# Splitting ordinary weight pieces with a casting and an accumulating DMA instead of VectorE's subtraction

## The chip, the cores and the metric

The kernel runs on one core of one Trainium2 chip. The metric is the device time of one execution in microseconds, lower is better. Before the change it is 1131.28 us, the median of three runs (1131.22 to 1131.42). Every profile is of one execution; its times are from the first instruction of the span.

## The reference

One encoder layer on 512 tokens of 1024 channels, all in float32: a half-step SwiGLU FFN, a mixing block with two attention branches, and a second half-step FFN. Each sub-layer is normalised before and after.

```python
f = _swiglu(_rmsnorm(x, ffn1_pre_g[l]), ffn1_w_gate[l], ffn1_w_up[l], ffn1_w_down[l])
x = x + 0.5 * _rmsnorm(f, ffn1_post_g[l])
h = _rmsnorm(x, mix_pre_g[l])
proj = h @ w_in[l]
qa, ka, va, qb, kb, vb, gate_a, gate_b = jnp.split(proj, splits, axis=-1)
ya = _neighbourhood_attention(...) @ w_branch_a[l]
yb = _dilated_mixture(...) @ w_branch_b[l]
merged = jax.nn.sigmoid(gate_a) * ya + jax.nn.sigmoid(gate_b) * yb
x = x + _rmsnorm(merged @ w_out[l], mix_post_g[l])
f = _swiglu(_rmsnorm(x, ffn2_pre_g[l]), ffn2_w_gate[l], ffn2_w_up[l], ffn2_w_down[l])
x = x + 0.5 * _rmsnorm(f, ffn2_post_g[l])
```

The FFN is `(silu(x @ w_gate) * (x @ w_up)) @ w_down` with an inner width of 2816. The neighbourhood branch has 8 heads, the dilated branch 12 heads in three groups. All weight matrices together are 196 pieces of 128 x 1024 numbers.

## The kernel before, in words

**Products.** TensorE multiplies in the type fp32r, which keeps fewer bits of a number than float32. So each operand is split into a high part (the number converted to fp32r) and a low part (the rest), and `mm3` (L152) makes three matmuls of each product: high by high, high by low, low by high (L153 to L155). A piece of weights feeds 24 matmuls with 512 columns each.

**Weights.** They lie in DRAM as 196 pieces of 512 KB in the order of use. Numbers in this document: 0 to 43 the first FFN's gate and up weights, 44 to 65 its w_down, 66 to 121 the mixing's input and branch weights, 122 to 129 w_out, 130 to 173 and 174 to 195 the second FFN's. Pieces 6 to 43 and 136 to 173 go through another routine (`seven`, with `load_blocks`), which adds blocks with accumulating DMAs of 256 KB from POOL's queue (L266, L267). Pieces 0 to 3 are split by hand at the start. The other 116 pieces are the ordinary ones; they come from `convert` (L97): SP loads the raw piece into one of two buffers `raw`, ScalarE converts it to the high part (L85), and VectorE subtracts the high part from the raw numbers for the low part (L86). Eight of the 116, the first four of the mixing and of the second FFN (`spread`), are kept in four half-size tiles each and are made early, during the product ahead of them.

**Lookahead.** The high and low tiles `w` share a pool of 12 buffers, that is six pieces. `take` (L131) hands a piece to TensorE and calls `fill`, so that five pieces stand ready or under way. The load of piece n+6 waits until TensorE has finished with piece n.

**Order.** In a few ranges (the norms between sub-layers) PE, ScalarE and VectorE run in the order in which the code is written, and SP does over the whole first FFN (L1013 to L1020). Everywhere else a scheduler sets the order in each engine's queue. The queue of each engine is worked off in order: an instruction that waits holds up all behind it.

**Norms.** `token_major` (L354) computes w_down or w_out for 4 token tiles. The second half of its product ends with a loop over the tiles: matmuls with the last four pieces, then sums of squares on ScalarE, `rstd_of` (L200 to L208; three small operations on POOL, L203, L206 and L207), scaling on VectorE, and for an earlier tile the transposes on TensorE (L221) that make the next sub-layer's input. Just ahead of that loop `fill(NPIECE)` (L395) asks for the next pieces.

Of the kernel before, what the change touches and what calls it, by code (L numbers as in the profile page):

```python
# [12 lines left out]
F32 = mybir.dt.float32  # L13
F32R = mybir.dt.float32r
BF16 = mybir.dt.bfloat16
AF = mybir.ActivationFunctionType
ALU = mybir.AluOpType
# [3 lines left out]
P = 128  # L21
# [8 lines left out]
PIECE = 1024  # L30
# [10 lines left out]
def block_kernel(ctx, tc, x, gains, weights, rpb_near, rpb_all, alibi0, alibi12, out):  # L41
    nc = tc.nc
# [3 lines left out]
    wp = ctx.enter_context(tc.tile_pool(name="wp", bufs=2 * NPIECE))  # L46
# [6 lines left out]
    halves = [slice(0, 512), slice(512, 1024)]  # L53

    def unit(dt=F32, name="u"):
        return up.tile([P, 512], dt, tag="u", name=name)
# [27 lines left out]
    def split(hi, lo, src):  # L84
        nc.scalar.copy(hi, src)  # L85
        nc.vector.tensor_tensor(lo, src, hi.bitcast(F32), op=ALU.subtract)  # L86
# [8 lines left out]
    spread = {b + i for b in (3 * NF, total - 3 * NF) for i in range(SPREAD)}  # L95

    def convert(n):  # L97
        raw = wp.tile([P, PIECE], F32, tag="raw", name="raw", bufs=2)
        nc.sync.dma_start(raw, weights[n])
        if n in spread:  # L100
            hi, lo = [[unit(F32R, "w"), unit(F32R, "w")] for _ in range(2)]
            for i, cs in enumerate(halves):
                split(hi[i], lo[i], raw[:, cs])
        else:
            hi, lo = [wp.tile([P, PIECE], F32R, tag="w", name="w") for _ in range(2)]
            split(hi, lo, raw)
            hi, lo = [[a[:, cs] for cs in halves] for a in (hi, lo)]
        pieces[n] = (hi, lo)

    def fetch():  # L110
        while state["next"] in pieces:
            state["next"] += 1
        if state["next"] < state["stop"]:
            convert(state["next"])
            state["next"] += 1
        else:
            state["ahead"]()
        for _ in range(2):
            if loads:
                loads.popleft()()  # L120
# [233 lines left out]
    def token_major(n_k, stat, g_post, f, g_pre, store, src=None):  # L354
# [18 lines left out]
        for k in range(n_k):  # L373
            if first == 0 and k % 2 and early:
                convert(early.pop(0))
            for t in range(NT):
                one(acc0[t], t, k, k, k == 0, k == n_k - 1)
# [4 lines left out]
        for k in range(first):  # L382
            if k > 2 and k % 2 == 0 and early:
                convert(early.pop(0))
            for t in range(NT):
                one(acc1[t], t, k, n_k + k, k == 0, False)
# [547 lines left out]
    for n in range(2, 4):  # L934
        raw = wp.tile([P, PIECE], F32, tag="raw", name="raw", bufs=2)
# [175 lines left out]
```

## Time and profile before

| what | before |
|---|---|
| median of three runs | 1131.28 us |
| the profiled execution's own time | 1130.41 us |
| its span | 1128.6 us |
| TensorE matmuls busy | 1113.6 us, 99% |
| VectorE busy | 720.1 us, 64% |
| ScalarE busy | 582.6 us, 52% |
| POOL busy | 99.7 us, 9% |
| granted TensorE clock, mean | 0.996 |
| DMA, SP's queue (hardware) | 134.96 MB, 37.7% of 16 engines |
| DMA, POOL's queue (software) | 19.93 MB, 11.2% of 16 engines |

A row of groups gives line, engine, operation, the tile written and read, sizes and count; then busy time and the mean in ns of one; then the idle time of the engine just before and what ended it. A row of waits gives who waited for whom, the total in us, how often, and the longest. A row of the timeline gives start and duration in us, engine, line and operation, and in brackets the idle time before it and its releaser. Matmuls overlap in the records: each is shown as 0.39 us, while they start 0.227 us apart.

### The profile page before, as it was taken

How to read it: one execution, taken by the hardware profiler on the slowest of the kernel's cores; microseconds unless marked ns; L12 is line 12 of the kernel's file. 1: busy time of each engine (PE TensorE's matmuls, PEld its weight loads, DVE VectorE, ACT ScalarE, POOL GpSimd, SP SyncE). 2: the span in 40 equal slices, each digit the busy share in tenths (PEclk: the TensorE clock that was granted, in tenths of full speed). 3: DMA queues.
4: the chain of work that ended last, by engine and by line, in shares of the span. 5: the costliest groups of instructions: out<-in, count | busy, mean ns of one | idle time of the engine just before them, and what ended most of it. 6: DMA issues, size and time to landing. Idle time of an engine off the chain costs nothing.

```text
span 1128.6 us, 18242 instructions
## 1 busy us (share of the span) xinstructions
PE 1113.6 (99%) x6956; PEld 1005.7 (89%) x6956; DVE 720.1 (64%) x1327; ACT 582.6 (52%) x1188; POOL 99.7 (9%) x157
## 2 busy tenths in 40 slices
PE   8999999999999999999999999999999999999997
PEld 6899999998888988888988888889899999998886
DVE  5797777773245677877486635655787777782312
ACT  5465555572233676767646632345555555571210
POOL 3111221000002000000000000013111111100001
PEclk8999999999999999999999999999999999999999
DMA  6789988443353353322223223353687677443511
GB/s 217 193 191 242 247 222 194 118 126 113 99 156 124 103 169 115 124 89 76 76 81 90 79 79 100 89 181 109 154 215 173 169 192 187 122 132 97 170 51 74
DMA packets 77430, 156.23 MB, mean 138 GB/s; under 512 B 22048, under 2 KB 24096, under 8 KB 77344
## 3 DMA queue, kind: packets, MB, share of 16 engines
q1 hardware_dynamic: 64000, 134.96, 37.7%
q0 software_dynamic: 10944, 19.93, 11.2%
q8 instruction: 54, 0.88, 0.3%
q10 hardware_dynamic: 2400, 0.20, 0.1%
q14 instruction: 32, 0.26, 0.1%
HBM read 150.02 MB, written 7.58 MB: 140 GB/s over the span
## 4 chain that ended last, share of the span: by engine, by line
PE 94%; DVE 2%; ACT 1%; DMA 1%; issue 0%; SPq 0%; DVEq 0%; POOLq 0%; POOL 0%; ACTq 0%
PE ps L153 18%; PE ps L154 18%; PE ps L155 18%; PE q L155 6%; PE q L154 6%; PE q L153 6%; PE p L155 3%; PE p L153 3%; PE p L154 3%; PE r L155 2%; PE r L153 2%; PE r L154 2%; PE ps L661 1%; PE ps L221 1%; PE ps L688 1%; PE ps L630 1%
## 5 line engine op out<-in xcount | busy, mean ns | idle before, releaser
L86 DVE TENSOR_TENSOR w<-raw,w 128x1024 fp32r<-128x1024 f32 (+1 forms) x200 | 195.0, 979 | 217.7 <-ACT w L85 211.4
L85 ACT CAST w<-raw 128x1024 fp32r<-128x1024 f32 (+1 forms) x200 | 169.6, 853 | 239.9 <-PE ps L154 162.8
L153 PE MATMUL ps<-hn_hi,w 128*128 128x512 f32 (+1 forms) x512 | 181.3, 355 | 0.0
L154 PE MATMUL ps<-hn_lo,w 128*128 128x512 f32 (+1 forms) x512 | 179.5, 351 | 0.0
L155 PE MATMUL ps<-hn_hi,w 128*128 128x512 f32 (+1 forms) x512 | 179.2, 350 | 0.0
L153 PE MATMUL ps<-w,u 128*128 128x512 f32 (+1 forms) x456 | 177.3, 389 | 0.0
L154 PE MATMUL ps<-w,u 128*128 128x512 f32 (+1 forms) x456 | 176.9, 388 | 0.0
L155 PE MATMUL ps<-w,u 128*128 128x512 f32 (+1 forms) x456 | 176.8, 388 | 0.0
L86 DVE TENSOR_TENSOR w<-t,w 128x512 fp32r<-128x512 f32 x152 | 104.3, 689 | 28.1 <-ACT w L85 28.1
L85 ACT CAST w<-t 128x512 fp32r<-128x512 f32 x152 | 93.7, 619 | 43.1 <-DVE t L272 18.4
L155 PEld LDWEIGHTS ps<-hn_hi,w 128*128 128x128 f32 x512 | 97.0, 189 | 12.8
L154 PEld LDWEIGHTS ps<-hn_lo,w 128*128 128x128 f32 x512 | 97.2, 190 | 11.6
L153 PEld LDWEIGHTS ps<-hn_hi,w 128*128 128x128 f32 x512 | 97.1, 190 | 11.8 <-issue 0.3
L155 PEld LDWEIGHTS ps<-w,u 128*128 128x128 f32 x456 | 85.7, 188 | 17.5
L154 PEld LDWEIGHTS ps<-w,u 128*128 128x128 f32 x456 | 85.7, 188 | 17.0
L153 PEld LDWEIGHTS ps<-w,u 128*128 128x128 f32 x456 | 85.7, 188 | 16.9
L155 PE MATMUL q<-hn_hi,w 128*128 128x256 f32 x304 | 86.4, 284 | 1.8 <-DVE w L86 1.8
L155 PE MATMUL p<-v,w 128*128 128x256 f32 x304 | 85.9, 284 | 0.9 <-DVE w L86 0.9
L154 PE MATMUL q<-v,w 128*128 128x256 f32 x304 | 86.2, 283 | 0.0
L153 PE MATMUL p<-v,w 128*128 128x256 f32 x304 | 86.2, 283 | 0.0
L155 PE MATMUL q<-v,w 128*128 128x256 f32 x304 | 86.2, 283 | 0.0
L154 PE MATMUL q<-hn_lo,w 128*128 128x256 f32 x304 | 86.2, 283 | 0.0
(149 smaller groups left out, 2299.8 us busy)
## 6 DMA issues: line engine op xcount, KB each, us to landing
raw<-in_weights_dram SPq DMA_DIRECT2D x156, 512.0 KB
t<-in_weights_dram SPq DMA_DIRECT2D x76, 256.0 KB
t<-in_weights_dram POOLq DMA_DIRECT2D x76, 256.0 KB, 5.5
w<-in_weights_dram SPq DMA_DIRECT2D x38, 256.0 KB
x<-in_x_dram SPq DMA_DIRECT2D x16, 256.0 KB
gain<-in_gains_dram SPq DMA_DIRECT2D x6, 512.0 KB
table<-bias_d SPq DMA_DIRECT2D x12, 256.0 KB
table<-in_alibi_dram SPq DMA_DIRECT2D x8, 256.0 KB
```

The source lines that it names most:

```text
L85: nc.scalar.copy(hi, src)
L86: nc.vector.tensor_tensor(lo, src, hi.bitcast(F32), op=ALU.subtract)
L153: nc.tensor.matmul(o, sh, mh, start=start, stop=False, **kw)
L154: nc.tensor.matmul(o, sh, ml, start=False, stop=False, **kw)
L155: nc.tensor.matmul(o, sl, mh, start=False, stop=stop, **kw)
L221: nc.tensor.transpose(pt[:, i * P:(i + 1) * P], xs[:, i * P:(i + 1) * P], ident)
L630: nc.tensor.matmul(ps[:, o:o + w], q[:, cols], windows(wide, kl, i), start=False, stop=True)
L661: nc.tensor.transpose(ps[:, i * P:(i + 1) * P], s, ident)
L688: nc.tensor.matmul(o, vv[n][:, h], m, start=first, stop=(n == 3 and part == 1), skip_group_check=True)
```

## The change

The tile `raw` and SP's load of it go from `convert`. A new routine `halve` makes both parts: a DMA from POOL's queue loads the piece straight into the high tile, of type fp32r, so that the DMA converts; ScalarE writes the negative of the high part into the low tile; a second DMA from POOL's queue reads the same weights from DRAM again and adds them to what stands in the low tile. Pieces of `spread` are made the same way in halves. The starting pieces 0 to 3, `load_blocks` and `split` elsewhere stay. Line numbers behind L97 grow by 6 in the changed kernel where they are not in `convert`.

```diff
     def convert(n):
-        raw = wp.tile([P, PIECE], F32, tag="raw", name="raw", bufs=2)
-        nc.sync.dma_start(raw, weights[n])
         if n in spread:
-            hi, lo = [[unit(F32R, "w"), unit(F32R, "w")] for _ in range(2)]
-            for i, cs in enumerate(halves):
-                split(hi[i], lo[i], raw[:, cs])
+            parts = [[unit(F32R, "w"), unit(F32R, "w")] for _ in halves]
+            for (hi, lo), cs in zip(parts, halves):
+                halve(hi, lo, weights[n][:, cs])
+            hi, lo = zip(*parts)
         else:
             hi, lo = [wp.tile([P, PIECE], F32R, tag="w", name="w") for _ in range(2)]
-            split(hi, lo, raw)
+            halve(hi, lo, weights[n])
             hi, lo = [[a[:, cs] for cs in halves] for a in (hi, lo)]
         pieces[n] = (hi, lo)
+
+    def halve(hi, lo, src):
+        nc.gpsimd.dma_start(hi, src)
+        nc.scalar.mul(lo, hi.bitcast(F32), -1.0)
+        nc.gpsimd.dma_start(lo, src, accum_op=ALU.add)
```

POOL's queue changes most, since it had few instructions. Ahead of the first norm (its first POOL operations write `ms` and `rstd` from the sums `ssf`) stood, before, the last accumulating loads of the first FFN's `seven`:

```order
L266 DMA t1_2881<-in_weights_dram 128x512
L267 DMA t3_2882<-in_weights_dram 128x512
L203 TENSOR_SCALAR ms0_4037<-ssf_3701 128x1
L206 TENSOR_SCALAR ms_4039<-ssf_3701,ms0_4037 128x1
L207 TENSOR_TENSOR rstd_4040<-ms_4039,mhalf_81 128x1
```

Now the same place of POOL's queue has the last pieces of w_down and the two behind them (L112 is the casting load into a high tile, and waits for TensorE to free it; L114 is the accumulating load into a low tile, whose number is one higher, and waits for ScalarE's negative):

```order
L112 DMA w_3896<-in_weights_dram 128x1024
L114 DMA w_3858<-in_weights_dram 128x1024
L112 DMA w_3925<-in_weights_dram 128x1024
L114 DMA w_3897<-in_weights_dram 128x1024
L114 DMA w_3926<-in_weights_dram 128x1024
L112 DMA w_3978<-in_weights_dram 128x1024
L114 DMA w_3979<-in_weights_dram 128x1024
L212 TENSOR_SCALAR ms_4013<-ssf_3685,ms0_4011 128x1
L213 TENSOR_TENSOR rstd_4014<-ms_4013,mhalf_81 128x1
```

All DMAs of pieces 44 to 71 stand ahead of the `rstd` of the first token tile, the last of them directly. The operation that began it, `ms0_4011`, has moved forward, and 22 rows of loads lie between the two.

In the mixing POOL had no work at all before; behind the norm's last `rstd` came the next norm's first operation:

```order
L206 TENSOR_SCALAR ms_4276<-ssx_4224,ms0_4274 128x1
L207 TENSOR_TENSOR rstd_4277<-ms_4276,mhalf_81 128x1
L203 TENSOR_SCALAR ms0_8030<-ssf_7948 128x1
L206 TENSOR_SCALAR ms_8032<-ssf_7948,ms0_8030 128x1
```

Now it holds two DMAs for every piece there. Pieces 101 to 105 (w_6436, w_6498, w_6560, w_6622 and w_6687 are their high tiles):

```order
L112 DMA w_6436<-in_weights_dram 128x1024
L114 DMA w_6219<-in_weights_dram 128x1024
L112 DMA w_6498<-in_weights_dram 128x1024
L114 DMA w_6437<-in_weights_dram 128x1024
L114 DMA w_6499<-in_weights_dram 128x1024
L112 DMA w_6560<-in_weights_dram 128x1024
L114 DMA w_6561<-in_weights_dram 128x1024
L112 DMA w_6622<-in_weights_dram 128x1024
L114 DMA w_6623<-in_weights_dram 128x1024
L112 DMA w_6687<-in_weights_dram 128x1024
L114 DMA w_6688<-in_weights_dram 128x1024
```

For pieces 100 to 102 the next cast stands ahead of the last accumulate; from 103 on, and for most pieces ahead of 100, each piece's cast and accumulate follow each other, so that the next piece's cast is issued only when this one's accumulate has been.

On ScalarE, in the stretch with the gates of the mixing, the cast of a piece (from `raw`) stood between the copies and conversions of the attention (`u`) and the sigmoid of the gates (`sig`):

```order
L704 COPY u_6779<-u_6780 64x512
L85 CAST u_6802<-ps_6797 128x256
L85 CAST w_6877<-raw_6875 128x1024
L85 CAST u_6805<-ps_6797 128x256
L887 ACTIVATE sig_6839<-ps_6808 128x512
L701 COPY u_6842<-ps_6843 128x256
```

Now the negative (L113) stands at such a place:

```order
L710 COPY u_6719<-u_6720 64x512
L85 CAST u_6742<-ps_6737 128x256
L113 ACTIVATE w_6750<-w_6749 128x1024
L85 CAST u_6745<-ps_6737 128x256
L893 ACTIVATE sig_6778<-ps_6748 128x512
L707 COPY u_6781<-ps_6782 128x256
```

What it waits for has changed: before, a load that SP had issued into one of two spare buffers; now the casting load, which is issued only after TensorE has freed the high tile.

## The prediction

> **What bounds the kernel now.** I read the busy times of the engines first, then who TensorE waited for, then the stretches, then single places.
>
> ```profile
> PE 1113.6 (99%) x6956; PEld 1005.7 (89%) x6956; DVE 720.1 (64%) x1327; ACT 582.6 (52%) x1188; POOL 99.7 (9%) x157
> PE ps L221 <- DVE u L960: 3.1, 1, 3.1
> PE q L155 <- DVE w L86: 1.8, 2, 1.2
> ...
> 250.00:310.00 60.00, 60.00 (x272) 49.92 (x271) 21.23 (x24) 18.68 (x29) 0.23 (x1) 1.00 0.34 106
> 600.00:650.00 50.00, 50.00 (x264) 42.95 (x264) 32.53 (x50) 32.90 (x58) 0.00 (x0) 1.00 0.26 81
> ```
>
> TensorE is busy for 99% of the span, and in two stretches taken from the middle (the columns are length, then PE, PEld, DVE, ACT and POOL busy, granted clock, DMA share, GB/s) for all of it. Its largest single wait is 3.1 us, at the start. So VectorE, which the change relieves, is not waited for: at most the 1.8 us in the second row and a few like it can be won. The question is whether the new way of making a piece still keeps TensorE fed. How fast TensorE takes pieces is seen in ScalarE's casts of them, for in most of these rows the cast waits for a buffer that TensorE lets go of:
>
> ```profile
> 401.39 1.05 ACT L85 CAST w<-raw 128x1024 fp32r<-128x1024 f32 x1
> ...
> 621.42 1.06 ACT L85 CAST w<-raw 128x1024 fp32r<-128x1024 f32 x1 [0.31 <-PE ps L154]
> 628.24 1.06 ACT L85 CAST w<-raw 128x1024 fp32r<-128x1024 f32 x1
> ...
> 716.51 1.05 ACT L85 CAST w<-raw 128x1024 fp32r<-128x1024 f32 x1 [0.47 <-PE ps L154]
> 721.95 1.05 ACT L85 CAST w<-raw 128x1024 fp32r<-128x1024 f32 x1 [4.39 <-PE ps L154]
> ```
>
> The row at 401.39 is piece 76, the one at 721.95 piece 126: 320.6 us for 50 pieces. While attention runs beside the projections a piece is taken every 6.8 us (621.42 to 628.24), without it every 5.44 us (716.51 to 721.95).
>
> **What goes.** 108 subtractions on VectorE, and 16 of half size:
>
> ```profile
> L86 DVE TENSOR_TENSOR w<-raw,w 128x1024 fp32r<-128x1024 f32 x108 | 132.3, 1225 | 176.7 <-ACT w L85 173.2 <-PE q L155 3.1
> L85 ACT CAST w<-raw 128x1024 fp32r<-128x1024 f32 x108 | 113.5, 1051 | 209.7 <-PE ps L154 162.4 <-DMA raw<-in_weights_dram 36.8 <-issue 5.9
> ```
>
> 132 us less for VectorE lie wholly beside TensorE's work and are worth nothing here. ScalarE's cast becomes a multiplication of the same shape; I leave it at 1.05 us. SP loses 116 loads of 512 KB, which cost it only issue time.
>
> **What comes: the price of two DMAs in a chain.** A piece now needs a casting load, ScalarE's negative, and an accumulating load, both DMAs issued by POOL in the order of its queue. The weights are read twice. The nearest rows are today's accumulating loads of 256 KB in the first FFN product (L266 and L267) and the plain loads of 512 KB on SP:
>
> ```profile
> q1 hardware_dynamic: 1722, 6.29, 33.5%
> raw<-in_weights_dram SPq DMA_DIRECT2D x12, 512.0 KB
> ...
> q0 software_dynamic: 2001, 3.64, 34.8%
> t<-in_weights_dram POOLq DMA_DIRECT2D x14, 256.0 KB, 4.7
> ...
> 856.42 0.86 POOL L266 DMA_DIRECT2D t<-in_weights_dram  x1 [8.97 <-DMA t<-in_weights_dram]
> 857.18 0.99 POOL L267 DMA_DIRECT2D t<-in_weights_dram  x1
> ...
> DMA to landing us min/median/max: 3.8/3.9/4.2
> DMA to landing us min/median/max: 5.1/5.6/6.7
> ```
>
> The first two rows are of the stretch 250 to 310 us: 33.5% of 60 us for 12 pieces is 1.68 us of all 16 DMA engines for one plain 512 KB load. The next two are of 900 to 970 us: 34.8% of 70 us for 3.64 MB, that is 13.9 accumulating loads of 0.262 MB, or 1.75 us each. The last two rows are the time from issue to landing in 840 to 900 us, of L266 and then of L267, which is issued 0.76 us behind it.
>
> - Accumulating 512 KB: no row. Below: 1.75 us, if the price is by row of 128 and not by byte. Above: the second of a pair lands 0.76 + 5.6 - 3.9 = 2.5 us after the first, so 4.9 us for twice the bytes. I take twice the engine time, **3.5 us**, for the engines' time is what queues up.
> - Casting load: no row. Below the plain load, 1.7 us; above the price of an accumulating one, 3.5 us. I take **1.7 us**: same bytes, same rows of 4 KB, nothing to read back. If the cast should do nothing (both types have 4 bytes), this price is right all the more.
> - What a DMA costs beside its data: 3.9 - 1.75 = 2.15 us, POOL's 0.86 us of issue in it.
>
> So a piece needs 5.2 us of the DMA engines, beside 1.7 now. How much of the chain overlaps is set by POOL's order:
>
> 1. *Interleaved* (the next cast ahead of the last accumulate, as in both second FFN products): 5.2 us a piece.
> 2. *Single* (cast, accumulate, cast, accumulate, most of the mixing): the next cast is issued right behind an accumulate and its data behind that one's; then ScalarE, then the next accumulate: 2.15 + 3.5 + 1.7 + 1.05 + 0.1 for the semaphores = 8.5 us a piece.
> 3. *Pairs* (two casts, two accumulates): 2.15 + 2 x 5.2 + 1.15 = 13.7 us, 6.85 us a piece.
>
> All are to be held against 5.44 and 6.8 us. Five pieces stand ready ahead of TensorE, so single delays are covered; a rate isn't.
>
> **The places.** Three stretches count, each from the first piece's release to a time at which TensorE needs the last:
>
> ```profile
> 229.23 1.05 ACT L85 CAST w<-raw 128x1024 fp32r<-128x1024 f32 x1
> ...
> 349.14 0.28 POOL L206 TENSOR_SCALAR ms<-ssf,ms 128x1 f32<-128x1 f32 x1 [45.46 <-ACT junk L195]
> ...
> 755.68 0.28 POOL L206 TENSOR_SCALAR ms<-ssf,ms 128x1 f32<-128x1 f32 x1 [3.67 <-ACT junk L195]
> ...
> 986.54 1.05 ACT L85 CAST w<-raw 128x1024 fp32r<-128x1024 f32 x1
> ...
> 1105.60 0.60 ACT L195 ACTIVATE junk<-ps 128x512 bf16<-128x512 f32 x1 [15.55 <-PE ps L155]
> ```
>
> - **First FFN's second product.** Piece 44 is cast at 229.23; the first norm's small POOL operation runs at 349.14. POOL's queue now has the DMAs of pieces 44 to 71 (22 of the product, four early ones in halves, two more) ahead of that operation, and the norm's scaling, transposes and TensorE's next projections stand behind it. 28 x 5.2 = 146 us against 119.9: **+26 us**.
> - **Mixing.** From piece 76 to 126 there are 50 steps: 15 of them in pairs (87 and 88, 93 and 94, 100 to 102, 116 and 117, 119 and 120, 122 to 125), 35 single: 35 x 8.5 + 15 x 6.85 = 400 us against 320.6. Then one more step, 8.5 us, to piece 127, and from its cast to the norm's POOL operation nine pieces' casts and eight pieces' accumulates (127 to 135, of which 130 to 133 are the next FFN's, in halves): 9 x 1.7 + 8 x 3.5 + 2.15 = 45 us. Together 454 us from 401.39, where it was 755.68 - 401.39 = 354.3: **+100 us**. I give nothing back for the five pieces of lead, since the norm waits for POOL's place in its queue and not for a piece; and ScalarE, in whose order each negative stands ahead of other work, is held up with POOL.
> - **Second FFN's second product.** From 986.54 to the last piece's first use. The block that ends at 1105.60 takes 5.44 us and meets the last piece a quarter before its end, so 1104: 117.5 us. Pieces 174 to 179 and 190 to 195 interleaved, 180 to 189 four single and six in pairs: 12 x 5.2 + 4 x 8.5 + 6 x 6.85 + 5 for the last landing = 142 us: **+25 us**.
> - **Start.** Pieces 4 and 5 get their negatives behind other ScalarE work; one accumulate more is in the way: **+1 us**.
>
> The sum is 26 + 100 + 25 + 1 = 152 us. The profiled execution took 1130.41 us (span 1128.6, 1.8 us around it), so 1282; the runs' median lies 0.9 us above it: **1283 us**.
>
> **A rule against a row.** The Trainium skill, "DMA: Bandwidth & Descriptors", section "Anatomy of one DMA — SWDGE (gpsimd) path", gives a DMA issued from GpSimd about 2.0 us plus its bytes over 436 GB/s. By that a 256 KB accumulate would take an estimated 2.6 us, where this trace has 3.9; a 512 KB DMA of either kind 3.2 us. That is rival 3 below.
>
> **Rivals.** One more row, of the stretch in which L266 and L267 run beside other loads (DMA share 0.77):
>
> ```profile
> 60.00:250.00 190.00, 190.00 (x1558) 188.80 (x1557) 148.96 (x255) 113.47 (x233) 28.16 (x32) 1.00 0.77 193
> ```
>
> 1. *The accumulate is cheap by rows, not bytes* (1.75 us for 512 KB). Then 3.45 us a piece interleaved, 6.75 single, 5.1 in pairs. The first FFN is covered (28 x 3.45 = 97 us of 120), the second too. The mixing keeps up at 6.8; where pieces go at 5.44, nine single steps lose 1.3 us each and eight paired ones win 0.3; the tail takes 38 us instead of 34. Some +14 us: 1145 us. For it: 144 packets of either size per load. Against: plain loads of 512 KB cost about what their bytes say.
> 2. *A DMA is dearer.* With 4.9 us for the accumulate: 6.6, 9.9 and 8.25 us a piece; +65, +183, +57, +1: 1437 us. With a cast at 3.5 us on top, 8.4, 11.7 and 10.05 us: +115, +291, +97, +1: 1635 us. For it: the spacing of the landings, and the DMA share of 0.77 in the row above. Against: those landings share the engines with other loads, which the mixing has few of.
> 3. *POOL's queue isn't late (no slower).* If an accumulate is in flight beside the next cast and does not hold it up, a single step is issue 0.86, landing 3.9 as now for 256 KB, 1.05 and 0.1: 5.9 us, and the five pieces of lead, 5 x 5.44 = 27 us, carry the 0.5 us by which it misses 5.44 in the nine single steps. Then TensorE never waits, and VectorE's relief may take the 1.8 us: 1130 us. It turns at 6.4 us a step, TensorE's own mean over the 50 steps (320.6 / 50). Against it: the landings of L266 and L267, which show that the second waits for the first.
>
> **How the numbers follow.** Forecast 0.50; rival 1 0.22; rival 2 0.20; rival 3 0.08. The range reaches down into rival 1, to 1165 us, and up to rival 2 with the dear accumulate alone, 1450 us; outside lie the lower half of rival 1, rival 3, and the dearest of rival 2, some 0.2. About 0.2% is what can be told from no change here. Slower than that takes the forecast, rivals 1 and 2, and a little of rival 3: 0.93; rival 3 is mostly within it: 0.05; faster 0.02.
>
> **What would show it.** TensorE's busy share falls to about 88%, and its waits name DMAs into w (L114) and, at the two norms, transposes of u (L221 becomes L227 in the changed numbering). POOL's issues of casts follow each other at about 8.5 us in the mixing, not at TensorE's 6.8 or 5.44. The software queue's share over the span should be near (116 x 5.2 + 76 x 1.75) / 1280 = 57% of the 16 engines, and the landing of an accumulate into w between 5 and 7 us. The norm's operation that stood at 349.14 should come near 376, that of 755.68 near 882. I am wrong if TensorE's share stays at 98% or more; if the accumulates land within 4 us (rival 1); or if the casts take as long as they do (rival 2).

## The result, and the profile after

The changed kernel takes **1273.68 us** (median of four runs, 1272.46 to 1275.65) where the kernel before takes 1131.25: a ratio of 1.1261 (1.1242 to 1.1281). The profiled execution took 1274.01 us, its span 1272.0, so 143.4 us more of span than before.

The page of the changed kernel, busy times and the software queue (packets, MB, share of 16 engines):

```profile
PE 1161.4 (91%) x6956; PEld 1032.1 (81%) x6956; DVE 584.8 (46%) x1203; ACT 581.6 (46%) x1188; POOL 275.4 (22%) x405
...
q0 software_dynamic: 46656, 141.58, 52.7%
```

VectorE has its 135 us less, and TensorE, which stood still for 15 us of the span before, now does for 111 us. Whom it waited for, and what POOL waited for in front of the accumulating loads (total us, times, and for TensorE the longest):

```profile
PE ps L160 <- DMA w<-in_weights_dram: 45.1, 15, 6.2
PE ps L227 <- DVE u L221: 10.4, 2, 8.7
...
  ACT w L113: 484.2, 92
```

The last row is from the view of L114: POOL stood 484 us, 92 times, in front of an accumulating load whose negative ScalarE had not made yet. All that is behind it in POOL's order stood with it. The places, in POOL's timeline of the changed kernel:

```profile
369.59 0.86 POOL L112 DMA_DIRECT2D w<-in_weights_dram  x1
377.41 0.85 POOL L114 DMA_DIRECT2D w<-in_weights_dram  x1 [6.96 <-ACT w L113]
378.02 0.58 POOL L212 TENSOR_SCALAR ms<-ssf,ms 128x1 f32<-128x1 f32 x1
...
432.46 0.91 POOL L112 DMA_DIRECT2D w<-in_weights_dram  x1
...
660.04 0.85 POOL L114 DMA_DIRECT2D w<-in_weights_dram  x1 [5.54 <-ACT u L85]
660.58 0.88 POOL L112 DMA_DIRECT2D w<-in_weights_dram  x1
668.04 0.85 POOL L114 DMA_DIRECT2D w<-in_weights_dram  x1 [6.58 <-ACT u L85]
668.58 0.87 POOL L112 DMA_DIRECT2D w<-in_weights_dram  x1
...
821.66 0.89 POOL L112 DMA_DIRECT2D w<-in_weights_dram  x1
...
869.47 0.64 POOL L212 TENSOR_SCALAR ms<-ssf,ms 128x1 f32<-128x1 f32 x1
...
1105.74 0.57 POOL L112 DMA_DIRECT2D w<-in_weights_dram  x1 [17.00 <-PE q L161]
```

The casting loads at 432.46, 821.66 and 1105.74 are those of pieces 76, 126 and 174. Set against the rows of before that the prediction shows (there a piece's time is ScalarE's cast, now it is the issue of its casting load; either comes when TensorE has freed the buffer or later):

| stretch | before, us | after, us | more | forecast |
|---|---|---|---|---|
| start to the first norm's operation | 349.1 | 378.0 | 28.9 | 27 |
| from there to piece 76 | 52.3 | 54.4 | 2.2 | 0 |
| piece 76 to piece 126, 50 steps | 320.6 | 389.2 | 68.6 | 79 |
| piece 126 to the second norm's operation | 33.7 | 47.8 | 14.1 | 20 |
| from there to piece 174 | 230.9 | 236.3 | 5.4 | 0 |
| piece 174 to the end of the span | 142.1 | 166.3 | 24.2 | 25 |

In the middle of the mixing (640 to 760 us) a casting load lands a median of 6.4 us after its issue and an accumulate 5.6 us; the rows are those of L112 and of L114:

```profile
DMA to landing us min/median/max: 4.7/6.4/7.2
DMA to landing us min/median/max: 5.3/5.6/8.5
```

ScalarE's negative between the two accumulates of the rows above:

```profile
666.69 1.06 ACT L113 ACTIVATE w<-w 128x1024 fp32r<-128x1024 f32 x1 [2.51 <-DMA w<-in_weights_dram]
```

It ends at 667.75, and the accumulate follows at 668.04. The row of POOL names a conversion (u L85) that ends in between, but the 0.3 us from negative to accumulate are the same at 377.41, where the row names the negative (from 376.06). So this step, 660.04 to 668.04, is 0.54 us from accumulate to casting load, 6.1 to its landing, 1.06 on ScalarE and 0.3 to the next issue: 8.0 us. On the mean over pieces 103 to 115 it is 8.3, as with the median landing of 6.4. By the medians the casting load's data comes only 0.54 + 6.4 - 5.6 = 1.3 us behind the accumulate's.

### The profile page after: what moved, and what is told of

Read it like the earlier page. It is cut to its first block, busy times and chain, and to the rows that moved or that the text cites. A ratio compares the mean times of both kernels' runs of the same rounds, so it can differ in the third digit from the quotient of the medians.

```text
span 1272.0 us, 18372 instructions
## 1 busy us (share of the span) xinstructions
PE 1161.4 (91%) x6956; PEld 1032.1 (81%) x6956; DVE 584.8 (46%) x1203; ACT 581.6 (46%) x1188; POOL 275.4 (22%) x405
## 3 DMA queue, kind: packets, MB, share of 16 engines
q0 software_dynamic: 46656, 141.58, 52.7%
## 4 chain that ended last, share of the span: by engine, by line
issue 41%; PE 37%; POOL 11%; DMA 6%; DVE 2%; ACT 2%; POOLq 0%; SPq 0%; DVEq 0%; ACTq 0%
POOL w L112 6%; DMA w<-in_weights_dram 5%; POOL w L114 5%; PE q L161 5%; PE q L159 5%; PE q L160 4%; PE ps L160 4%; PE ps L159 4%; PE ps L161 4%; PE p L161 2%; PE p L159 2%; PE p L160 2%; PE r L161 1%; PE r L160 1%; PE r L159 1%
## 5 line engine op out<-in xcount | busy, mean ns | idle before, releaser
L113 ACT ACTIVATE w<-w 128x1024 fp32r<-128x1024 f32 (+1 forms) x124 | 123.4, 1002 | 398.5 <-DMA w<-in_weights_dram 375.5
L114 POOL DMA_DIRECT2D w<-in_weights_dram x124 | 110.5, 914 | 570.9 <-ACT w L113 484.2
L160 PE MATMUL ps<-w,u 128*128 128x512 f32 (+1 forms) x456 | 188.5, 413 | 45.1 <-DMA w<-in_weights_dram 45.1
L159 PE MATMUL ps<-hn_hi,w 128*128 128x512 f32 (+1 forms) x512 | 184.2, 361 | 3.4 <-DVE u L514 3.4
L159 PE MATMUL ps<-w,u 128*128 128x512 f32 (+1 forms) x456 | 186.0, 408 | 1.0 <-DMA w<-in_weights_dram 1.0
L161 PE MATMUL ps<-w,u 128*128 128x512 f32 (+1 forms) x456 | 185.9, 408 | 0.0
L161 PE MATMUL ps<-hn_hi,w 128*128 128x512 f32 (+1 forms) x512 | 181.5, 355 | 0.0
L160 PEld LDWEIGHTS ps<-w,u 128*128 128x128 f32 x456 | 91.2, 200 | 71.2 <-DMA w<-in_weights_dram 52.8
L85 ACT CAST w<-t 128x512 fp32r<-128x512 f32 x152 | 93.8, 620 | 46.0 <-DVE t L278 21.2
L112 POOL DMA_DIRECT2D w<-in_weights_dram x124 | 99.3, 876 | 59.7 <-PE q L161 41.5
L159 PEld LDWEIGHTS ps<-hn_hi,w 128*128 128x128 f32 x512 | 98.8, 193 | 16.2 <-DVE u L514 3.8
L161 PEld LDWEIGHTS ps<-hn_hi,w 128*128 128x128 f32 x512 | 98.6, 193 | 13.7
L159 PEld LDWEIGHTS ps<-w,u 128*128 128x128 f32 x456 | 91.5, 201 | 21.1 <-DMA w<-in_weights_dram 1.6
L161 PEld LDWEIGHTS ps<-w,u 128*128 128x128 f32 x456 | 91.4, 200 | 18.7
L272 POOL DMA_DIRECT2D t<-in_weights_dram x38 | 34.9, 922 | 281.2 <-DVE w L86 124.7
L161 PE MATMUL q<-hn_hi,w 128*128 128x256 f32 x304 | 86.2, 284 | 1.8 <-DVE w L86 1.8
L161 PE MATMUL p<-v,w 128*128 128x256 f32 x304 | 85.8, 283 | 0.9 <-DVE w L86 0.9
L159 PE MATMUL q<-hn_hi,w 128*128 128x256 f32 x304 | 86.1, 283 | 0.5 <-DVE up L337 0.5
L86 DVE TENSOR_TENSOR u<-ps,u 128x256 fp32r<-128x256 f32 (+3 forms) x92 | 46.1, 513 | 86.9 <-ACT u L85 86.2
```

Source lines behind the costliest of these rows:

```text
L112: nc.gpsimd.dma_start(hi, src)
L113: nc.scalar.mul(lo, hi.bitcast(F32), -1.0)
L114: nc.gpsimd.dma_start(lo, src, accum_op=ALU.add)
L159: nc.tensor.matmul(o, sh, mh, start=start, stop=False, **kw)
L160: nc.tensor.matmul(o, sh, ml, start=False, stop=False, **kw)
L161: nc.tensor.matmul(o, sl, mh, start=False, stop=stop, **kw)
```

## The experiments

Each comparison is with the kernel before on the same chip (1130.75 to 1130.89 us). POOL's order in each kernel is its own, since a scheduler lays it out; where that matters it is said.

**Order: the negative and the accumulate behind the next piece's casting load.** All bytes and all DMAs stay.

```diff
     def halve(n, hi, lo, src):
         nc.gpsimd.dma_start(hi, src)
-        nc.scalar.mul(lo, hi.bitcast(F32), -1.0)
-        nc.gpsimd.dma_start(lo, src, accum_op=ALU.add)
+        held.append((n, hi, lo, src))
...
         pieces[n] = (hi, lo)
+        finish(1)   # mul and accumulate of all held pieces but the last one
```

> Edit: the negative and the accumulating load of a piece are issued behind the casting load of the next piece; every DMA stays, and every byte. Theory (the chain in POOL's order sets 8.3 us a piece in the mixing, the DMA engines set about 5 us a piece in the second FFN products): the mixing keeps up with TensorE again, its +85 us go to about 0 to +10, and the two second products keep +29 and +24, so about 1185 us (1165 to 1200). Rival 'the weights are read twice, the traffic is the loss': nothing changes, 1255 us or more. Rival 'ScalarE stands still in front of negatives': falls as in the theory; the run with VectorE tells that one apart.

Measured: 1154.39 us, a ratio of 1.0205 (1.0175 to 1.0235): 119 of the 142 us are back, more than the theory's range of 1165 to 1200 us has. POOL's timeline of this kernel (L114 is now the casting load, L123 the accumulate, L223 the norms' operation):

```profile
353.54 0.28 POOL L223 TENSOR_SCALAR ms<-ssf,ms 128x1 f32<-128x1 f32 x1 [8.52 <-ACT junk L212]
...
674.95 0.55 POOL L114 DMA_DIRECT2D w<-in_weights_dram  x1 [3.73 <-PE ps L172]
675.81 0.85 POOL L123 DMA_DIRECT2D w<-in_weights_dram  x1 [0.31 <-ACT w L122]
680.39 0.55 POOL L114 DMA_DIRECT2D w<-in_weights_dram  x1 [3.73 <-PE ps L172]
...
775.35 0.28 POOL L223 TENSOR_SCALAR ms<-ssf,ms 128x1 f32<-128x1 f32 x1 [3.47 <-ACT junk L212]
...
1126.93 0.28 POOL L223 TENSOR_SCALAR ms<-ssf,ms 128x1 f32<-128x1 f32 x1 [14.32 <-ACT junk L212]
```

Casting loads follow each other at 5.44 us and wait for TensorE: POOL keeps TensorE's pace. That the loss is the traffic falls. But so does a part of the theory: the first norm comes 4.4 us late instead of 28.9, and from the second norm to the last product's first norm operation it takes 351.6 us, where before took 350.8 (1106.45 - 755.68 in POOL's timeline). The second products were not held by the engines' time either. Most of the 23 us that are left lie in the mixing: its end, the second norm, comes 19.7 us late.

**VectorE makes the negative.** `nc.scalar.mul(lo, ...)` becomes `nc.vector.tensor_scalar_mul(lo, ...)`.

> Edit: VectorE makes the negative in place of ScalarE; the order of POOL's queue stays nearly the same. Theory (POOL's chain): the step stays near 8.3 us, 1265 to 1285 us. Rival 'ScalarE stands still in front of the negatives and holds up gates and attention': ScalarE is free, the mixing's +85 us go, 1200 us or less.

Measured: 1288.70 us, ratio 1.1392 (1.1359 to 1.1425), a little above the range. Freeing ScalarE wins nothing. POOL's timeline of this kernel:

```profile
688.32 0.86 POOL L112 DMA_DIRECT2D w<-in_weights_dram  x1
696.01 0.86 POOL L114 DMA_DIRECT2D w<-in_weights_dram  x1 [6.83 <-PE ps L161]
696.56 0.88 POOL L112 DMA_DIRECT2D w<-in_weights_dram  x1
```

The step is 8.2 us still. From piece 115 to 126 it is 7.2 us where the change has 6.2: POOL's order has fewer pairs there. A wait of ScalarE for loads, 375 us in the changed kernel, is thus not a price of its own.

**The second load without the addition.** `accum_op=ALU.add` goes from the last line of `halve`.

> Edit: the second load of a piece is a casting load too, without the addition, so that the low part is wrong (it holds the weights instead of the remainder); issues, waits, order and bytes read stay. Theory with the accumulate's price at twice a plain load's (3.5 against 1.7 us): a single step falls from 8.3 to about 6.6 us and an interleaved one to 3.4 us, so both second products lose nothing and the mixing a little: about 1145 us (1132 to 1165). Rival 'reading the weights twice is the loss': 1255 us or more. Rival 'the price is the issue and the fixed latency of each DMA': 1240 us or more.

Measured: 1153.67 us, ratio 1.0199 (1.0133 to 1.0264). The page's row of the software queue, and the landings of both loads in 640 to 760 us, first L112, then L114:

```profile
q0 software_dynamic: 46656, 141.58, 45.7%
...
DMA to landing us min/median/max: 4.4/5.0/7.3
DMA to landing us min/median/max: 3.8/4.0/6.5
```

Same packets and bytes as in the changed kernel, and the same order in POOL's queue, but the second load lands 1.6 us sooner, and the first, which stands behind it, 1.4 us. Only the 1.4 us shorten the step, since the next step waits for the landing of the first load and not of the second. Two casting loads of single steps, in POOL's timeline:

```profile
653.17 0.54 POOL L112 DMA_DIRECT2D w<-in_weights_dram  x1
...
660.07 0.54 POOL L112 DMA_DIRECT2D w<-in_weights_dram  x1
```

That is 6.9 us, the mean over pieces 103 to 115 too, where the change has 8.3. The first norm comes 1.6 us late, the mixing loses 11 us more and the last product 4. Reading twice is therefore not the loss; what the addition puts into the chain is most of it.

**No second load.** The last line of `halve` goes.

> Edit: the accumulating load is left out, so that the low part is wrong (the negative of the high part). Theory: POOL's queue holds casting loads only, each issued when TensorE frees a buffer; 1.7 us of the DMA engines a piece; as before, 1128 to 1134 us. Rival 'it is the casting load that is dear (3.5 us of the engines)': the software queue's share shows it, and the first norm still comes late, 1140 us or more.

Measured: 1131.45 us, ratio 1.0007 (0.9996 to 1.0018). Its page and the landing of L112 in 640 to 760 us:

```profile
PE 1111.7 (98%) x6956; PEld 1004.1 (89%) x6956; DVE 585.4 (52%) x1203; ACT 583.8 (52%) x1188; POOL 164.1 (15%) x281
...
q0 software_dynamic: 28800, 80.75, 30.3%
...
DMA to landing us min/median/max: 2.9/4.0/5.8
```

Two readings. VectorE is relieved as in the change, and the time is the kernel's before: there was nothing to win. And the prices of a load by the engines' time: the software queue took 0.303 x 1129.6 = 342 us here, 0.457 x 1148.6 = 525 with a second casting load, 0.527 x 1272.0 = 670 with the accumulate. Over 116 pieces that is **1.6 us** for a casting load and **2.8 us** for an accumulate of 512 KB, 4.4 together. Taken against the kernel before (0.112 x 1128.6 = 126 us), the first casting load comes to (342 - 126) / 116 = 1.9 us, and both DMAs to 4.7. So these prices hold to some 0.3 us.

**The casting load's part given back to SP and ScalarE.** SP loads the raw piece, ScalarE makes the high part and then the negative, POOL issues accumulates only.

```diff
     def convert(n):
+        raw = wp.tile([P, PIECE], F32, tag="raw", name="raw", bufs=2)
+        nc.sync.dma_start(raw, weights[n])
...
-        nc.gpsimd.dma_start(hi, src)
+        nc.scalar.copy(hi, raw)
```

> Edit: the raw piece comes by SP's plain load as in the kernel before, ScalarE makes the high part and its negative from it, and POOL issues the accumulating load alone; bytes and accumulates stay as in the change. Theory (a casting load that stands behind an accumulate that stands behind a casting load, in one queue, makes the step; the engines' time, 4.4 us a piece, is not the bound): no load waits in POOL's queue, so nearly as with the order changed: 1131 to 1165 us, 1145 taken. Rival 'the accumulate itself is the loss, in whatever queue the other load stands': 1220 us or more. Rival 'ScalarE': it has 1.05 us more a piece, 116 x 1.05 = 122 us, all beside TensorE's work if the theory holds.

Measured: 1174.25 us, ratio 1.0384 (1.0363 to 1.0405): most of the loss is gone, but 9 us more than the range allowed. ScalarE's timeline of this kernel:

```profile
365.55 1.05 ACT L112 CAST w<-raw 128x1024 fp32r<-128x1024 f32 x1 [11.71 <-DMA raw<-in_weights_dram]
...
736.27 1.05 ACT L112 CAST w<-raw 128x1024 fp32r<-128x1024 f32 x1 [2.79 <-PE ps L160]
741.71 1.05 ACT L112 CAST w<-raw 128x1024 fp32r<-128x1024 f32 x1 [1.78 <-PE ps L160]
```

In the mixing pieces come at TensorE's 5.44 us in these rows, and the 50 steps from piece 76 take 329 us (before 321), so an accumulate in POOL's queue hardly hurts where no load stands in line with it. The miss lies mainly ahead of the norms: ScalarE, in its own order, stands in front of raw loads, which have two buffers, while accumulates fill the engines (share 0.96 in 300 to 370 us). The first norm comes 19.4 us late, the second another 21.5, of which 10 lie behind piece 126. The queue that blocks was exchanged for another one. What each of the two, the buffers and the engines' time, has in these losses was not tried.

**The accumulate in two halves.** Two of 256 KB, one behind the other, in place of one of 512 KB.

> Edit: the accumulating load of a whole piece is issued as two of 256 KB, one behind the other; same bytes, twice the rows and issues. If the price goes by bytes (2.8 us of the engines for 512 KB): POOL issues one DMA more a piece, 0.55 to 0.85 us in a single step: 1273 plus some 50 x 0.7 and a little at the second products, 1300 to 1325 us, and the software queue's time on the engines stays at about 670 us. If it goes by rows or a fixed part (1.75 us for 256 KB, so 3.5 for two): 0.7 us of the engines more a piece on top, the software queue's time at about 745 us, 1330 to 1370 us. Rival 'the split lets the engines work side by side': no longer than 1273 us.

Measured: 1273.87 us, ratio 1.1265 (1.1221 to 1.1309): no dearer, which none but the last rival had. POOL's timeline and the queue's row of this kernel (L115 are the halves):

```profile
q0 software_dynamic: 62208, 141.59, 54.5%
...
662.25 1.74 POOL L115 DMA_DIRECT2D w<-in_weights_dram  x2 [6.97 <-ACT u L85]
663.33 1.22 POOL L112 DMA_DIRECT2D w<-in_weights_dram  x1
671.70 1.73 POOL L115 DMA_DIRECT2D w<-in_weights_dram  x2 [7.15 <-ACT u L85]
```

A single step is dearer, 9.45 us in these rows. But POOL's order was laid out anew with 7 pairs from piece 103 to 126 instead of 4, and the mean step from 115 to 126 fell from 6.2 to 5.5 us. The total is therefore a sum of two opposite effects and settles neither. The queue's time does settle one thing: 0.545 x 1267.3 = 691 us against 670, 0.2 us for each of the 108 DMAs more, where a price by rows would have added 0.7. The price goes nearly by bytes.

**The changed order, with the eight spread pieces made the old way.** To the first experiment's edit comes, in `convert`, the old code for every n in `spread`.

> Edit: the order of the earlier run (negative and accumulate behind the next piece's casting load) with the eight spread pieces (66 to 69, 130 to 133) made the old way. Theory: what that order still lost (4 us ahead of the first norm, 15 in the mixing, nearly all of it from 735 us on, where those pieces' loads stand bunched ahead of the second norm at a DMA share over 1) is the engines' time there; four pieces less, at 2.8 us of accumulate each, give back 11 us or more: 1133 to 1145 us, 1138 taken. Rival 'the rest is lost elsewhere': 1150 us or more. Faster than the kernel before is expected by none, since without any accumulate the time was the kernel before's.

Measured: 1140.37 us, ratio 1.0087 (1.0070 to 1.0104): as the theory had it. Here TensorE still waited once for long. The timelines of VectorE and of ScalarE's queue in this kernel, and TensorE's largest wait:

```profile
579.80 0.17 DVE L851 TENSOR_TENSOR joint<-joint 128x16 f32<-128x16 f32 x1 [8.41 <-DMA joint<-stats]
...
567.65 0.38 ACTq L848 DMA_DIRECT2D joint<-stats  x1
...
PE ps L693 <- DVE u L681: 7.6, 1, 7.6
```

A load of 48 KB, issued by ScalarE at 567.65, was awaited until 579.80, and TensorE's next matmuls with it. The load itself was late: the last packet of the three such loads on ScalarE's queue ended at 579.44.

**Pieces 99 to 103 made the old way as well.** These are the ones whose loads were in flight at that time.

```diff
-        return n not in spread
+        return n not in spread and not 99 <= n <= 103
```

> Edit: the run with the order changed and the spread pieces made the old way, with pieces 99 to 103 made the old way as well. In that run TensorE still waited 7.6 us once, for the probabilities that VectorE scales, and VectorE 8.4 us for a small load of 48 KB (the joint statistics), issued at 567.7 while casting loads and accumulates of pieces 99 to 103 were in flight. Theory: the small load's packets stand behind those of the weights, and without these loads there the 7.6 us go: 1131 to 1135 us. Rival 'that wait comes from VectorE's or ScalarE's order': 1138 us or more.

Measured: **1129.88 us**, ratio 0.9993 (0.9984 to 1.0003). The view of L848 (who waited for it) and the page of this kernel:

```profile
  DVE joint L851: 0.4, 1
...
PE 1112.3 (99%) x6956; PEld 1004.7 (89%) x6956; DVE 601.3 (53%) x1224; ACT 582.0 (52%) x1188; POOL 244.3 (22%) x363
```

VectorE's wait for the three small loads fell from 11.2 to 0.4 us, and TensorE is busy for 99%. The last packet of these loads now ends at 571.21, 2.9 us after the last issue. With 103 of the 116 pieces made by DMAs in another order, the loss is gone entirely, and still nothing is won. The time is 1 us below the theory's range: 10.5 us were gained where one wait of 7.6 was to go, and the rest was not followed up.

**The mixing's pieces made the old way.** Pieces 72 to 129 by the old code, the rest as in the change.

> Edit: pieces 72 to 129, those of the mixing, are made the old way; pieces 4, 5, 44 to 71, 130 to 135 and 174 to 195 as in the change. If the losses of the stages stand for themselves: 29 us ahead of the first norm, 24 in the last product, the mixing's go but for the spread pieces ahead of the second norm (0 to 10): 1184 us (1175 to 1195). Rival 'the loss is passed on': a late first norm delays the mixing's start by the same amount only where the mixing is slow itself, 1150 us or less when it is caught up.

Measured: 1192.50 us, ratio 1.0546 (1.0524 to 1.0567). The norms' operations of this kernel in POOL's timeline:

```profile
376.26 0.58 POOL L227 TENSOR_SCALAR ms<-ssf,ms 128x1 f32<-128x1 f32 x1
...
788.11 0.60 POOL L227 TENSOR_SCALAR ms<-ssf,ms 128x1 f32<-128x1 f32 x1
...
1166.21 0.28 POOL L227 TENSOR_SCALAR ms<-ssf,ms 128x1 f32<-128x1 f32 x1 [8.34 <-ACT junk L216]
```

This is inside the range. 27.1 us late at the first norm, 5.3 us more between the norms, 27.3 us more behind the second: the losses of the stages add up, and nothing is caught up later.

**Every piece of the mixing alone, and then with a longer chain.** POOL is held to the order of the code from the start of the mixing to its last product; the second kernel adds a second negative behind the first.

```diff
-    ... + [(0, state["sp"], (mybir.EngineType.SP,))]:
+    ... + [(0, state["sp"], (mybir.EngineType.SP,)), (state["sp"], state["mx"], (mybir.EngineType.Pool,))]:
...
         nc.scalar.mul(lo, hi.bitcast(F32), -1.0)
+        nc.scalar.mul(lo, hi.bitcast(F32), -1.0)   # the second kernel only
```

> Edit: POOL's queue keeps the order in which the code is written from the start of the mixing to its last product, so that every piece from 72 to about 125 is cast, accumulate, cast, accumulate, with no pairs; nothing else. Theory (8.3 us for a single step, 6.2 where pairs are mixed in): some 15 steps of the mixing's last part go from 6.2 to 8.3 us, +25 to +35 us, 1295 to 1310 us. Rival 'TensorE or the DMA engines set the pace, not the order': 1273 us.

> Edit: the run before with ScalarE's negative made twice, one behind the other, so 1.06 us more in each piece's chain, no byte more. Theory: a single step goes from 8.3 to 9.4 us, seen in the spacing of the casting loads; 50 steps, +50 to +60 us over that run in the mixing alone. Rival 'the DMA engines set the step': the spacing stays 8.3 us, since ScalarE is idle most of it.

Measured: 1318.74 us, ratio 1.1663 (1.1640 to 1.1686), and 1360.85 us, ratio 1.2035 (1.2010 to 1.2060). POOL's timeline, of the first kernel and of the second, at pieces 119 and 120 and at pieces 113 and 114:

```profile
812.43 0.87 POOL L112 DMA_DIRECT2D w<-in_weights_dram  x1
...
821.02 0.88 POOL L112 DMA_DIRECT2D w<-in_weights_dram  x1
```

```profile
819.38 0.88 POOL L112 DMA_DIRECT2D w<-in_weights_dram  x1
...
828.82 0.88 POOL L112 DMA_DIRECT2D w<-in_weights_dram  x1
```

From piece 115 to 126 the mean step is 6.19 us in the change, 8.40 without pairs, 9.44 with 1.06 us more on ScalarE. The last three of the 9.44 have halves of the next FFN's pieces between them; from 115 to 123, without halves, it is 8.30 and 9.29. The step takes the added time about one for one: the chain of load, negative and accumulate sets it, not the engines' time. The first kernel's total is 9 us above its range: its whole mixing, with three pairs gone ahead of piece 115 too, is slower (piece 76 to 126 in 426 us, not 389).

The second kernel's total misses too: it is 42 us above the first's, where the mixing alone was to take 50 to 60 us more. From the first norm to the second it does take 72 us more. But from the second norm to the end it takes 25 us less, and POOL's order there, which was not held, shows why for the last product: of the three kernels only this one has it interleaved to its end. From piece 174's casting load to the norm's operation behind it are 126.4 us, in the first kernel 139.5, in the change 139.9, before 119.9 from the cast of 174. Interleaved, the last product loses 6.5 us instead of 20, although its chain is longer.

## Why the prediction was right, and where its working was not

1283 us was forecast, 1273.7 came. The reason given for the largest term holds; two of the steps are right in size for a wrong reason.

**No gain from VectorE: right.** The kernel without accumulates has VectorE at 52% and the time of before.

**The price of the DMAs: the sum right, its parts not.** The accumulate was to land after 2.15 + 3.5 = 5.65 us; it lands after 5.6. But its time on the engines is 2.8 us and not 3.5, the rest 2.8 and not 2.15. The casting load was taken at 1.7 and measures 1.6 to 1.9. A piece needs 4.4 to 4.7 us of the engines, not 5.2, and so the software queue's share came to 52.7% and not 57%. The term that was off is "twice the engine time" of the 256 KB accumulates of before: two of 256 KB in place of one of 512 KB take 2.8 + 0.2 = 3.0 us together, not 3.5. That the 1.75 us were read in a stretch shared with other queues is the likely reason, not a shown one.

**Single steps: right, and for the reason given.** 8.5 us forecast, 8.3 measured, 8.4 with the order held; the casting load lands after 4.0 us without accumulates, 5.0 behind a plain second load and 6.4 behind an accumulate; pairs 6.85 forecast, while the mixture from piece 115 on, with four pairs in POOL's order, takes 6.2. Hence 389 us for 50 steps and not 400. Behind them 14 us more came instead of 20.

**Both second products: the size right, the step wrong.** "28 x 5.2 = 146 us against 119.9" made the engines the bound, with all pieces interleaved. The run with the order changed moves the same bytes and loses 4.4 us there instead of 28.9. What the changed kernel shows: pieces 44 to 51 go at 4.5 us, as interleaved pieces should. The last ones don't: between the casting loads of 56 and 71 lie 79 us for eleven pieces and three halves, 6.3 us a piece. POOL's order there is cast, accumulate, accumulate, or two casts and two accumulates, with halves between, and POOL mostly stands in front of an accumulate 6 to 9 us at a time. Too dear a price and too fast an order cancelled: that 28.9 us came where 26 was forecast is luck. The last product is the same: 3.8 us a piece from 174 to 180, where 5.2 was taken, and 6.5 from 189 to 195, where 5.2 was taken too. Interleaved to its end, in the kernel with the longer chain, it loses 6.5 us up to the norm's operation.

**ScalarE "held up with POOL": no price of its own.** VectorE's negative left the step as it was.

**What was left out.** 5.4 us behind the second norm, and 2.2 us behind the first. Most of the 5.4 is POOL's order once more. Behind the second norm an accumulate stands between the first and the second of eight `rstd` operations (POOL's timeline of the changed kernel; the first `rstd` is at 870.47):

```profile
875.76 0.92 POOL L114 DMA_DIRECT2D w<-in_weights_dram  x1 [4.17 <-ACT w L113]
...
877.74 0.57 POOL L213 TENSOR_TENSOR rstd<-ms,mhalf 128x1 f32<-128x1 f32 x1
```

So the eight take 26.3 us from the first to the last, 21.8 before (756.04 to 777.81): 4.6 us more. The 8.7 us for which TensorE waited at L227 lie here. The 2.2 us stay open.

TensorE's share came to 91% instead of 88% since its busy time rose from 1113.6 to 1161.4 us. In two stretches of the changed kernel (columns as in the prediction, the clock third from the end):

```profile
350.00:400.00 50.00, 40.49 (x172) 31.99 (x171) 14.71 (x22) 16.05 (x35) 14.84 (x31) 0.80 0.59 133
...
850.00:900.00 50.00, 33.87 (x168) 28.41 (x169) 20.21 (x31) 21.61 (x51) 19.26 (x38) 0.80 0.72 177
```

The granted clock is 0.80 in these two, in which TensorE waits, and 1.00 in the prediction's rows of before. Behind the wait of 6.2 us matmuls start 0.43 us apart from 860.48 to 864.32, and 0.23 us apart from 865.10 on. What this adds to the loss was not tried.

**The rivals.** Rival 1, an accumulate that goes by rows, falls: 0.2 us for a DMA more of the same bytes, and a landing after 5.6 us, not within 4. Rival 2 falls: neither DMA comes near its 4.9 and 3.5 us of the engines. Rival 3, that POOL is not late, falls: 92 waits for 484 us. The Trainium skill's "DMA: Bandwidth & Descriptors", section "Anatomy of one DMA — SWDGE (gpsimd) path", belongs to it, with an estimated 3.2 us for 512 KB. Measured are 4.0 us for a casting load with no accumulates about (2.9 at the least) and 5.6 for an accumulate: the estimate is nearer for the load, and that section has no term for the addition.

## What to carry to other kernels

Where a DMA has to wait for another engine's work on an earlier DMA's data, and both are issued from one in-order queue, price the step by the whole chain (here 0.5 + 6.4 + 1.1 us and the semaphores, 8.3 us for 4.4 to 4.7 us of engine time), and issue the next piece's first DMA ahead of this piece's second: that alone took 119 of 142 us back without a byte less. Read the order piece by piece down to the end of a stage, and not only at its start, since what was interleaved in the first half was not in the second. And ask first whether the engine that is relieved is waited for: the best version here is equal to the kernel before, 1129.88 against 1130.83 us.

## What had not been expected

A **small load on another queue** comes late when accumulates and casting loads are in flight. Of the three loads of 48 KB in the run with the spread pieces made the old way, the last, issued at 567.65, was awaited until 579.80, 12 us later; with pieces 99 to 103 off the software queue the three together were waited for 0.4 us instead of 11.2. The packets themselves were late: the last ended 11.8 us after that issue, 2.9 with these pieces off the queue, and 1.8 in the kernel before (571.42, issued at 569.63). That removal also changed VectorE's and ScalarE's order around that place a little; that the small packets stood behind the large ones is the likely reading, not a shown one.

The **accumulate of 512 KB** takes 2.8 us of the engines where a casting load of the same bytes takes 1.6 to 1.9, and lands 1.6 us later than it, with equal packets and bytes counted by the queue (46656 and 141.58 MB in both kernels).
